# A hymba encoder block on one core: the negated row maxima added to the last three score pairs of a unit by accumulating DMAs, and the loads of q, K and V issued on the sync queue

## The chip, the cores and the metric

The kernel runs on one core of one Trainium2 chip. The metric is the device time of one execution in microseconds (us). The kernel before the change was run three times: the median is 2271.43 us, the lowest 2271.02 and the highest 2275.55. One further execution was profiled.

## The reference, cut to what matters

The program is one encoder layer for 2048 tokens and 16 meta tokens with a model width of 1024, all in float32. A projection of the normalised input gives queries (4 heads of 128), keys and values (2 heads of 128 each) and the input of a Fourier branch. The change lies in the attention of two query heads over one key and value head:

```python
def attend(qb):
    s = jnp.einsum('bkgqd,bksd->bkgqs', qb, kt).astype(jnp.float32) * scale
    p = jax.nn.softmax(s, axis=-1).astype(vt.dtype)
    return jnp.einsum('bkgqs,bksd->bkgqd', p, vt)
```

After that come the normalised outputs of attention and Fourier branch, an output projection added to the input, and a feed-forward part of width 4096.

## The kernel before, in words

A tile framework writes one queue of instructions for each engine: it takes the operations of the Python program, plans them by costs of its own, and so decides the order in which each engine runs them. On the chip each engine works through its queue strictly in that order and waits at an instruction until its operands are there. A change in one place can therefore move instructions on all engines.

Matrix products are mostly done three times over (helper `mm3`, lines 77 to 82): each operand is split into a high and a low part, and three products are added in one PSUM bank.

Attention runs beside the Fourier branch first (names `pa`, `py`, its last `py` at 497 us of the profiled span), then beside the output projection of the Fourier half (`pof`, 507 to 777 us), then beside that of the attention half (`poa`, 784 to 1019 us). It consists of 16 units; a unit is 256 queries of two heads, 512 columns, against all 2064 keys. The keys come in 16 tiles of 128 and one last tile of meta tokens.

- `scores(u, i)` makes one score tile on TensorE (PE) with three products, and ScalarE (ACT) copies it out of PSUM (line 780). Only two PSUM banks serve these tiles (`bufs=2`), so the third product from here waits for the copy of the first. Two tiles stand side by side in one pair `S` of 128x1024 in SBUF; a unit has eight pairs, 0 to 7. A running maximum `M` is kept on VectorE (DVE) at line 786.
- `stats(u)` turns the maxima of a unit into `mb`, the maximum of each of the 512 columns on all 128 partitions (line 811, a copy from PSUM on ACT).
- `softmax(u, i)` goes over the pairs: DVE subtracts `mb` from the pair (line 840), ACT takes the exponential (line 841), DVE adds the pair into `acc` (lines 845 and 847), and PE multiplies it by the values (line 849, name `o`, four matmuls a pair). These products of a unit stand in the order of the pairs.
- The scores run 20 tiles ahead of the softmax (`LEADT = 3` beyond one unit), so that `mb` of a unit is there about when the softmax of the unit before it ends.

The operands come from DRAM: `load_q` (line 738), `load_k` (704) and `load_v` (710 and 713), all issued by GpSimd (POOL). POOL also computes reciprocal square roots (line 192, names `rs_f`, `rs_m`, `rs_a`) and small additions (line 954). All other transfers of these stages are issued by the sync engine (SP): the tables of the Fourier branch (line 539, name `traw`), inputs, weights, and stores.

Of the kernel before, what the change touches and what calls it, by code (L numbers as in the profile page):

```python
# [13 lines left out]
AF = mybir.ActivationFunctionType  # L14
ALU = mybir.AluOpType
# [4 lines left out]
P = 128  # L20
# [11 lines left out]
NT = SEQ // P  # L32
# [3 lines left out]
MR = 96  # L36
# [13 lines left out]
P_BUFS = 5  # L50
S_BUFS = 11
A_BUFS = 5
ORDER = "1265734"
ISQ = 1.0 / math.sqrt(HD)


def f32v(ap):
    return ap.bitcast(F32)
# [26 lines left out]
def ins_of(x):  # L85
    return getattr(x, "ins", x)


def bc(ap, shape):
    return ap.broadcast_to(shape)  # L90
# [45 lines left out]
def encoder_block(ctx: ExitStack, tc: tile.TileContext, x, meta, w_in, w_f,  # L136
                  w_out, w_up, w_down, g_fin, g_cols, g_rows, c_id, c_rope, c_dft, c_even, c_odd, c_rem, out):
    nc = tc.nc
# [56 lines left out]
    q_d = [dram.tile([P, 2, NQ, 256], F32, name=f"q_d{b}") for b in range(8)]  # L195
    k_d = dram.tile([P, NKV, 2, SEQ + MR], F32, name="k_d")
    v_n = dram.tile([P, NKV, NT, P], F32, name="v_n")
    v_m = dram.tile([MR, NKV, P], F32, name="v_m")
    h_d = [dram.tile([P, D], F32, name=f"h_d{t}") for t in range(NT)]
    m_d = [dram.tile([P, KT, 512], F32, name=f"m_d{b}") for b in range(4)]  # L200
    f_d = {n: dram.tile([P, 2, 4, 512], F32, name=f"f_d{n}") for n in ORDER}

# [491 lines left out]
    def misc(name, shape=(P, 512)):  # L694
        return app.tile(list(shape), F32, name=name, tag="misc")


    KC = 4 * P
    KCP = 640

    def load_k(u, g, c):
        n = KC + (MR if c == 3 else 0)
        kt = ap.tile([P, 2, KCP if c == 3 else KC], R32, name=f"kt_{u}_{c}", tag=f"KT{c // 3}", bufs=1 if c == 3 else 3)
        nc.gpsimd.dma_start(kt[:, :, :n], k_d[:, g, :, c * KC:c * KC + n])
        return kt

    def load_v(u, g, c):
        if c == 4:
            vt = ap.tile([P, P], R32, name=f"vm_{u}", tag="VM", bufs=1)
            nc.gpsimd.dma_start(vt[:MR], v_m[:, g])  # L710
        else:
            vt = ap.tile([P, 4, P], F32, name=f"vn_{u}_{c}", tag="VT", bufs=4)
            nc.gpsimd.dma_start(vt, v_n[:, g, 4 * c:4 * c + 4])
        return vt

    o_d = [dram.tile([P, 2, NQ, 512], F32, name=f"o_d{b}") for b in range(4)]
# [12 lines left out]
    def attention():  # L729
# [5 lines left out]
        def load_q(u):  # L735
            b, g = units[u]
            q = ap.tile([P, 2, 2, 256], R32, name=f"q_{u}", tag="q", bufs=2)
            nc.gpsimd.dma_start(q, q_d[b][:, :, 2 * g:2 * g + 2])
            return q.rearrange("p l h n -> p l (h n)")

        def start(u, q=None):
            q = load_q(u) if q is None else q
            state[u] = dict(q=(q[:, 0], q[:, 1]), S=[], k=KV["k", u])
# [3 lines left out]
        def loads(kind, u, c):  # L747

            if u and units[u][1] == units[u - 1][1]:
                KV[kind, u] = KV[kind, u - 1]  # L750
            else:
                KV.setdefault((kind, u), []).append((load_v if kind == "v" else load_k)(u, units[u][1], c))
# [37 lines left out]
        def over_keys(x, name, op):  # L790

            ps = misc("pm_" + name, (P, 4, P))
            for a in range(4):
                nc.tensor.transpose(ps[:, a], x[:, a * P:(a + 1) * P], ident)
            r = ap2.tile([P, 4], F32, name="mx_" + name, tag="mx", bufs=2)
            nc.vector.tensor_reduce(r, ps, axis=AX.X, op=op)
            return r

        def rows_to_cols(vec, name):

            ps = misc("pd_" + name, (P, 4, P))
            for a in range(4):
                nc.tensor.transpose(ps[:, a], bc(vec[:, a:a + 1], [P, P]), ident)
            return ps.rearrange("p a e -> p (a e)")

        def stats(u):
            s = state[u]
            r = over_keys(s["M"], f"m{u}", ALU.max)
            yield
            mb = s["mb"] = ap2.tile([P, 512], F32, name=f"mb_{u}", tag="mb", bufs=2)  # L810
            nc.scalar.copy(mb, rows_to_cols(r, f"m{u}"))  # L811

        def softmax(u, i):

            s = state[u]
            nm = f"{u}_{i}"
            vt = KV["v", u]
            if i == NT:
                S = s["S"][-1][:MR]
                nc.vector.tensor_tensor(S, S, s["mb"][:MR], op=ALU.subtract)  # L820
                nc.scalar.activation(S, S, AF.Exp, scale=ISQ)
                hi = ap2.tile([P, 512], R32, name="ph_" + nm, tag="ph", bufs=1)
                acc = s["acc"]
                nc.scalar.copy(hi[:MR], S)
                nc.vector.tensor_tensor(hi[32:64], S[32:64], f32v(hi[32:64]), op=ALU.subtract)
                sm = s["sum"] = ap2.tile([P, 512], F32, name=f"sum_{u}", tag="pl", bufs=1)
                nc.vector.tensor_tensor(sm, acc[:, 0], acc[:, 1], op=ALU.add)
                nc.vector.tensor_tensor(sm[:META], sm[:META], S[:META], op=ALU.add)
                nc.tensor.matmul(s["O"], vt[4][:MR], hi[:MR], start=False, stop=True)
                return  # L830
            j = i // 2
            S = s["S"][j]
            if i == 0:
                s["acc"] = ap2.tile([P, 2, 512], F32, name=f"acc_{u}", tag="acc", bufs=1)
                s["O"] = app.tile([P, 512], F32, name=f"o_{u}", tag="O")
            acc = s["acc"]
            p = S
            if i % 2 == 0:
                mb = s["mb"].rearrange("p (o n) -> p o n", o=1).broadcast_to([P, 2, 512])
                nc.vector.tensor_tensor(S, S, mb, op=ALU.subtract)  # L840
                nc.scalar.activation(p, S, AF.Exp, scale=ISQ)  # L841
                return
            v = vt[j // 2]
            if j == 1:
                nc.vector.tensor_tensor(acc, s["S"][0], p, op=ALU.add)
            elif j > 0:
                nc.vector.tensor_tensor(acc, acc, p, op=ALU.add)
            for e in range(2):
                nc.tensor.matmul(s["O"], v[:, 2 * j % 4 + e], p[:, e], start=i + e == 1, stop=False)  # L849

        def finish(u):
# [25 lines left out]
            else:  # L877
                for h in range(2):
                    nc.vector.tensor_tensor(sqs[b], sqs[b], O[:, h * 256:(h + 1) * 256], op=ALU.add)

        q0 = load_q(0)
        for c in range(4):
            loads("k", 0, c)
# [7 lines left out]
        def more(upto):  # L891
            while ahead[0] < min(upto, total):
                w, i = divmod(ahead[0], K)
                if i == K // 2 and w < len(units) - 1:
                    start(w + 1)
                scores(w, i)
                loads_next("k", w, i)
                ahead[0] += 1
                if i == NT:
                    later.append(stats(w))  # L900
# [6 lines left out]
        for n in range(total):  # L907
            u, i = divmod(n, K)
            for g in list(later):
                if next(g, "end") == "end":  # L910
                    later.remove(g)
            softmax(u, i)
            loads_next("v", u, i)
            if i == NT:
                later.append(finish(u))
                next(later[-1])
            more(n + 1 + K + LEADT)
            yield
# [102 lines left out]
    def a_tile(name, dt=F32):  # L1021
        return mp.tile([P, 512], dt, name=name, tag="a", bufs=A_BUFS)

# [182 lines left out]
    def up_pass(p, sp, pc, UW, ready, first, hs, beside):  # L1206
# [8 lines left out]
        for g in range(8):  # L1215
            X, Y, p1, u2, p5, C = ({} for _ in range(6))

            def keep(name, q, t):
                nc.sync.dma_start(s_d[g // 2][:, ORDER.index(name), 2 * (g % 2) + q], t)

            for name in ORDER:
                hi, lo = ready.pop(0)
# [81 lines left out]
    def down_pass(p, sp, FIRST, hs):  # L1304
# [36 lines left out]
        def down_operands():  # L1341

            for g in range(4):
                raw, S, loads = {}, {}, []

                def stationary(name):
                    S[name] = []
                    for h in range(2):
                        r = dn.tile([P, 2, 512], F32, name=f"a{name}_{p}_{g}_{h}", tag="ar", bufs=a_bufs)
                        eng = nc.sync if g else nc.gpsimd  # L1350
                        loads[:] = [ins_of(eng.dma_start(r, s_d[g][:, ORDER.index(name), 2 * h:2 * h + 2]))]
                        S[name].append(r)
# [119 lines left out]
        for g in range(4):  # L1472
            X, Y = {}, {}
            last = g == 3
            for name in ORDER:
                (a0, b0), (a1, b1) = (lambda f: ((f[0], f[1]), (f[2], f[3])))(ready.pop(0))
# [255 lines left out]
```

## Time and profile before

| | before |
|---|---|
| median of 3 runs | 2271.43 us |
| the profiled execution's own time | 2272.19 us |
| its span, first to last instruction | 2270.4 us |
| PE busy | 2240.4 us |
| DVE busy | 1693.0 us |
| ACT busy | 1177.8 us |
| POOL busy | 248.0 us |
| clock granted to TensorE | 0.997 |

A time in the profile is counted from the first instruction of the span. "x" is how many instructions a group holds. In a group of instructions the mean length of one is given in ns, then the idle time of the engine ahead of them and what ended it. A matmul's row is longer than the time that it takes from the next one, since matmuls overlap: rows of 390 ns start 227 ns after each other. Rows with an engine's name and a q (SPq, POOLq) belong to that engine's queue, where transfers are issued.

### The profile page before, as it was taken

The numbers are of one execution on the slowest core, as the hardware profiler recorded it, in microseconds if no ns is written. First come the engines' busy times: TensorE is split into PE (matmuls) and PEld (weight loads), VectorE is DVE, ScalarE is ACT, GpSimd is POOL, SyncE is SP. The second block draws the span as 40 slices with busy tenths as digits, with TensorE's granted clock in tenths as the row PEclk, the third lists the DMA queues.
The fourth block names the chain that finished last, engine by engine and source line by source line (L and its number), as shares of the span: only waits on it lengthen the run. The fifth ranks groups of instructions, "written<-read, shape, count | busy, mean of one in ns | idle before, by whom it ended". The sixth has DMA issues, their size and how long they took to land.

```text
span 2270.4 us, 28121 instructions
## 1 busy us (share of the span) xinstructions
PE 2240.4 (99%) x10238; PEld 1774.5 (78%) x10238; DVE 1693.0 (75%) x2250; ACT 1177.8 (52%) x1997; POOL 248.0 (11%) x285
## 2 busy tenths in 40 slices
PE   9999999999999999999999999999999999999998
PEld 7888987766667666677888878888878888788887
DVE  6334589999999888888676669679655656696795
ACT  6443366665555566668555644334445555443343
POOL 2212120003223122010000020000200000200000
PEclk9999999999999999999999999999999999999999
DMA  5332252133343524367777575444674444864442
GB/s 203 89 107 77 78 157 81 51 94 113 101 155 116 192 90 136 126 254 243 254 233 237 201 275 192 158 133 149 227 311 166 156 151 155 306 201 157 128 138 84
DMA packets 191786, 367.40 MB, mean 162 GB/s; under 512 B 15760, under 2 KB 74768, under 8 KB 189984
## 3 DMA queue, kind: packets, MB, share of 16 engines
q1 hardware_dynamic: 171040, 310.08, 40.4%
q0 software_dynamic: 20464, 55.27, 7.7%
q8 instruction: 80, 1.31, 0.2%
q14 instruction: 58, 0.48, 0.1%
q10 hardware_dynamic: 144, 0.26, 0.0%
HBM read 236.28 MB, written 129.27 MB: 161 GB/s over the span
## 4 chain that ended last, share of the span: by engine, by line
PE 88%; DVE 7%; ACT 2%; issue 2%; POOL 1%; DMA 1%; POOLq 0%; DVEq 0%; ACTq 0%; SPq 0%
PE o L849 7%; PE ux L82 5%; PE ux L80 5%; PE ux L81 5%; PE dx L80 5%; PE dx L81 5%; PE dx L82 5%; PE uy L82 4%; PE uy L81 4%; PE uy L80 4%; PE dy L82 4%; PE dy L80 4%; PE dy L81 4%; PE s L80 2%; PE s L82 2%; PE s L81 2%
## 5 line engine op out<-in xcount | busy, mean ns | idle before, releaser
L849 PE MATMUL o<-S,vn 128*128 128x512 f32 x512 | 243.6, 596 | 4.2 <-ACT S L841 3.5
L70 ACT CAST ah<-a 128x1024 fp32r<-128x1024 f32 x108 | 112.9, 1050 | 259.8 <-PE dx L81 105.3
L80 PE MATMUL dx<-bh,ah 128*128 128x512 f32 x496 | 192.6, 388 | 1.3 <-DVE hs L1493 1.3
L780 ACT COPY S<-s 128x512 f32<-128x512 f32 x256 | 145.0, 584 | 91.9 <-PE s L82 72.5
L82 PE MATMUL dx<-bh,al 128*128 128x512 f32 x496 | 192.5, 388 | 0.0
L81 PE MATMUL dx<-bl,ah 128*128 128x512 f32 x496 | 192.5, 388 | 0.0
L80 PE MATMUL ux<-bf,wuh 128*128 128x512 f32 x448 | 176.0, 393 | 3.2 <-ACT wuh L70 3.1
L82 PE MATMUL ux<-bf,wul 128*128 128x512 f32 x448 | 175.4, 392 | 0.7 <-DVE wul L71 0.7
L81 PE MATMUL ux<-bf,wuh 128*128 128x512 f32 x448 | 175.4, 391 | 0.0
L840 DVE TENSOR_TENSOR S<-S,mb 128x1024 f32<-128x1024 f32 x128 | 155.2, 1227 | 11.8 <-ACT mb L811 11.7
L841 ACT ACTIVATE S<-S 128x1024 f32<-128x1024 f32 x128 | 135.1, 1063 | 43.3 <-DVE S L840 42.2
L80 PE MATMUL dy<-bh,ah 128*128 128x512 f32 (+1 forms) x388 | 151.5, 390 | 3.5 <-ACT ah L70 3.5
L82 PE MATMUL dy<-bh,al 128*128 128x512 f32 (+1 forms) x388 | 151.3, 390 | 1.6 <-DVE al L71 1.6
L71 DVE TENSOR_TENSOR al<-a,ah 128x1024 fp32r<-128x1024 f32 x108 | 131.1, 1220 | 27.2 <-ACT ah L70 26.9
L81 PE MATMUL dy<-bl,ah 128*128 128x512 f32 (+1 forms) x388 | 151.2, 390 | 0.0
L849 PEld LDWEIGHTS o<-S,vn 128*128 128x128 f32 x512 | 92.2, 189 | 75.1 <-issue 59.0
L80 PE MATMUL s<-q,kt 128*128 128x512 f32 (+1 forms) x272 | 145.1, 534 | 2.8 <-ACT S L780 2.4
L71 DVE TENSOR_TENSOR bl<-d,bh 128x1024 fp32r<-128x1024 f32 x92 | 112.1, 1219 | 21.5 <-ACT bh L70 21.5
L80 PE MATMUL uy<-bf,wuh 128*128 128x512 f32 x320 | 125.0, 391 | 0.3 <-ACT wuh L70 0.3
L82 PE MATMUL uy<-bf,wul 128*128 128x512 f32 x320 | 124.6, 390 | 0.7 <-DVE wul L71 0.7
L786 DVE TENSOR_TENSOR M<-M,S 128x1024 f32<-128x1024 f32 x96 | 117.6, 1225 | 9.9 <-ACT S L780 9.0
L81 PE MATMUL uy<-bf,wuh 128*128 128x512 f32 x320 | 124.8, 390 | 0.0
(323 smaller groups left out, 5663.2 us busy)
## 6 DMA issues: line engine op xcount, KB each, us to landing
a<-s_d SPq DMA_DIRECT2D x84, 512.0 KB, 3.7
R<-in_w_up_dram SPq DMA_DIRECT2D x32, 1024.0 KB, 5.5
s_d<-s SPq DMA_DIRECT2D x128, 256.0 KB, 2.1
s_d<-c SPq DMA_DIRECT2D x96, 256.0 KB, 2.8
d<-in_w_down_dram SPq DMA_DIRECT2D x48, 512.0 KB, 5.1
f_d<-lf SPq DMA_DIRECT2D x56, 256.0 KB, 2.8
bf<-f_d SPq DMA_DIRECT2D x7, 2048.0 KB, 13.5
a<-s_d POOLq DMA_DIRECT2D x24, 512.0 KB, 5.3
```

What stands on the lines that cost most here:

```text
L70: self.high = nc.scalar.copy(hi, src)
L71: self.low = nc.vector.tensor_tensor(lo, src, f32v(hi), op=ALU.subtract)
L80: nc.tensor.matmul(out, a[0], b[0], start=first, stop=False, skip_group_check=chain)
L81: nc.tensor.matmul(out, a[0], b[1], start=False, stop=False, skip_group_check=chain)
L82: nc.tensor.matmul(out, a[1], b[0], start=False, stop=last, skip_group_check=chain)
L780: nc.scalar.copy(S[:, i % 2], ps)
L786: nc.vector.tensor_tensor(M, M, S, op=ALU.max)
L840: nc.vector.tensor_tensor(S, S, mb, op=ALU.subtract)
L841: nc.scalar.activation(p, S, AF.Exp, scale=ISQ)
L849: nc.tensor.matmul(s["O"], v[:, 2 * j % 4 + e], p[:, e], start=i + e == 1, stop=False)
```

## The change

A constant `FAR = 5` is added. `mb` is now made with its sign turned, and added where it was subtracted. For the pairs 0 to 4 and for the last tile DVE does that as before. For the pairs 5, 6 and 7 DVE does nothing any more: `stats` issues three DMAs on POOL's queue that add `mb` into these pairs in SBUF, 512 KB of destination each, as soon as `mb` is there. The exponential of these pairs waits for its DMA. The loads of q, K and V go from POOL's queue to SP's.

```diff
+FAR = 5
 ...
-        nc.gpsimd.dma_start(kt[:, :, :n], k_d[:, g, :, c * KC:c * KC + n])
+        nc.sync.dma_start(f32v(kt[:, :, :n]), k_d[:, g, :, c * KC:c * KC + n])
 ...
-            nc.gpsimd.dma_start(vt[:MR], v_m[:, g])
+            nc.sync.dma_start(f32v(vt[:MR]), v_m[:, g])
 ...
-            nc.gpsimd.dma_start(vt, v_n[:, g, 4 * c:4 * c + 4])
+            nc.sync.dma_start(vt, v_n[:, g, 4 * c:4 * c + 4])
 ...
-            nc.gpsimd.dma_start(q, q_d[b][:, :, 2 * g:2 * g + 2])
+            nc.sync.dma_start(f32v(q), q_d[b][:, :, 2 * g:2 * g + 2])
 ...
-            nc.scalar.copy(mb, rows_to_cols(r, f"m{u}"))
+            nc.scalar.activation(mb, rows_to_cols(r, f"m{u}"), AF.Copy, scale=-1.0)
+            for S in s["S"][FAR:NT // 2]:
+                nc.gpsimd.dma_start(S, bc(mb.rearrange("p (o n) -> p o n", o=1), [P, 2, 512]), accum_op=ALU.add)
 ...
-                nc.vector.tensor_tensor(S, S, s["mb"][:MR], op=ALU.subtract)
+                nc.vector.tensor_tensor(S, S, s["mb"][:MR], op=ALU.add)
 ...
-                mb = s["mb"].rearrange("p (o n) -> p o n", o=1).broadcast_to([P, 2, 512])
-                nc.vector.tensor_tensor(S, S, mb, op=ALU.subtract)
+                if j < FAR:
+                    mb = bc(s["mb"].rearrange("p (o n) -> p o n", o=1), [P, 2, 512])
+                    nc.vector.tensor_tensor(S, S, mb, op=ALU.add)
                 nc.scalar.activation(p, S, AF.Exp, scale=ISQ)
```

With the change the planner also writes other orders. Two places matter below. A name such as `S_10_6424` is a pair by its first key tile (`S_10` is pair 5, `S_12` pair 6, `S_14` pair 7) with a serial number that only tells instances apart; in `s_4` the number is the key tile. The lines in the changed kernel are one to four higher: 780 is 781 there, 811 is 812, 841 is 845.

On ACT, from `mb` of unit 9 on (at 702.90 us in the profile of before), the kernel before has:

```order
L811 COPY mb_6565<-pd_m_6566 128x512
L780 COPY S_0_6541<-s_1_6575 128x512
L855 COPY O_6589<-o_6286 128x512
L780 COPY S_2_6595<-s_2_6591 128x512
L841 ACTIVATE S_0_6216<-S_0_6216 128x1024
L780 COPY S_2_6595<-s_3_6610 128x512
L841 ACTIVATE S_2_6248<-S_2_6248 128x1024
L841 ACTIVATE S_4_6318<-S_4_6318 128x1024
L70 CAST ohl_6649<-O_6589 128x512
L780 COPY S_4_6663<-s_4_6659 128x512
L780 COPY S_4_6663<-s_5_6667 128x512
```

And the changed kernel at the same place on ACT:

```order
L812 ACTIVATE mb_6565<-pd_m_6566 128x512
L781 COPY S_0_6541<-s_1_6578 128x512
L859 COPY O_6592<-o_6289 128x512
L781 COPY S_2_6598<-s_2_6594 128x512
L845 ACTIVATE S_0_6216<-S_0_6216 128x1024
L781 COPY S_2_6598<-s_3_6613 128x512
L845 ACTIVATE S_2_6251<-S_2_6251 128x1024
L845 ACTIVATE S_10_6424<-S_10_6424 128x1024
L845 ACTIVATE S_4_6321<-S_4_6321 128x1024
L845 ACTIVATE S_12_6465<-S_12_6465 128x1024
L71 CAST ohl_6652<-O_6592 128x512
L845 ACTIVATE S_14_6481<-S_14_6481 128x1024
```

The exponentials of the pairs 5, 6 and 7 have moved ahead of those of the pairs 2 to 4 and ahead of the copies of the next unit's score tiles 4 and 5, which follow in the next rows. In the kernel before, exponentials stand in the order of the pairs, and eleven copies of score tiles stand between `mb` and that of pair 7 in this unit; now there are three. The other units have moved in the same way: by the order, 9 to 19 such copies stood there in the units 0 to 14, now 3 to 5 and in unit 13 seven. The last unit has no copies behind it in either kernel.

On SP, before the first unit, the kernel before has stores and the tables of the Fourier branch:

```order
L454 DMA k_d<-kt_3398 512x1x96
L539 DMA traw_0_4049<-c_odd 128x516
L539 DMA traw_1_4055<-c_odd 128x516
L539 DMA traw_2_4061<-c_odd 128x516
L539 DMA traw_3_4067<-c_odd 128x516
```

And the changed kernel at the same place on SP:

```order
L455 DMA k_d<-kt_3398 512x1x96
L540 DMA traw_0_4052<-c_odd 128x516
L540 DMA traw_1_4058<-c_odd 128x516
L540 DMA traw_2_4064<-c_odd 128x516
L739 DMA q_3566<-q_d_102 128x2x512
L705 DMA kt_0_3568<-k_d 128x2x512
L705 DMA kt_1_3570<-k_d 128x2x512
```

The first loads of q and K, which stood at the head of POOL's queue, now stand behind three table loads on SP.

## The prediction

> **What bounds the kernel now.** I read the page first: busy times, the chain that ended last, the costliest groups.
>
> ```profile
> span 2270.4 us, 28121 instructions
> ...
> PE 2240.4 (99%) x10238; PEld 1774.5 (78%) x10238; DVE 1693.0 (75%) x2250; ACT 1177.8 (52%) x1997; POOL 248.0 (11%) x285
> ...
> PE 88%; DVE 7%; ACT 2%; issue 2%; POOL 1%; DMA 1%; POOLq 0%; DVEq 0%; ACTq 0%; SPq 0%
> ...
> L780 ACT COPY S<-s 128x512 f32<-128x512 f32 x256 | 145.0, 584 | 91.9 <-PE s L82 72.5
> ...
> L840 DVE TENSOR_TENSOR S<-S,mb 128x1024 f32<-128x1024 f32 x128 | 155.2, 1227 | 11.8 <-ACT mb L811 11.7
> L841 ACT ACTIVATE S<-S 128x1024 f32<-128x1024 f32 x128 | 135.1, 1063 | 43.3 <-DVE S L840 42.2
> ```
>
> TensorE is the bound: busy for 99% of the span and 88% of the chain. The share of DVE says nothing about single stages, so next I asked for the stretches of the span in which attention runs, and for the heavy stretch in which it starts.
>
> ```profile
> core 0: us, PE busy (x) PEld busy (x) DVE busy (x) ACT busy (x) POOL busy (x), PEclk, DMA share, GB/s
> 340.00:640.00 300.00, 295.21 (x1283) 202.96 (x1282) 293.29 (x364) 186.40 (x312) 56.37 (x54) 1.00 0.30 92
> 640.00:1000.00 360.00, 356.13 (x1429) 244.48 (x1428) 313.57 (x395) 217.82 (x357) 70.96 (x61) 1.00 0.41 137
> 320.00:340.00 20.00, 19.96 (x123) 17.48 (x122) 16.16 (x29) 15.47 (x30) 4.23 (x8) 1.00 0.98 293
> ```
>
> Between 340 and 640 us DVE is nearly as full as PE (293.3 against 295.2 of 300 us). The change takes load from it there. But PE is idle for only 4.8 us in the first stretch (300 - 295.21) and 3.9 us in the second (360 - 356.13): 8.7 us is about all that a lighter DVE can give.
>
> **The change part by part.** *DVE.* Three pairs in 16 units, 48 subtractions of 1.227 us, are 58.9 us of DVE work that goes. DVE is on the chain for 7%, but PE cannot get back more than its 8.7 us of gaps, and a part of these ends with POOL or with transfers. I take 5 us off, with 0 and 8.7 as bounds. The turned sign and additions in place of subtractions cost nothing: as many instructions of the same size.
>
> *The wait on ACT.* ACT works in order, and its order has changed: in unit 9 the exponentials of the pairs 5, 6 and 7 now stand right behind that of pair 1, each waiting for its DMA. So what counts is not when these pairs are needed, but what stands behind the waiting exponential: the copies of the next unit's scores. I work unit 9 out from its rows on ACT and PE.
>
> ```profile
> 702.90 0.59 ACT L811 COPY mb<-pd_m 128x512 f32<-128x512 f32 x1 [1.22 <-PE pd_m L803]
> ...
> 706.45 2.25 ACT L841 ACTIVATE S<-S 128x1024 f32<-128x1024 f32 x2
> 710.10 0.62 ACT L70 CAST ohl<-O 128x512 fp32r<-128x512 f32 x1 [1.39 <-DVE O L861]
> 711.26 1.27 ACT L780 COPY S<-s 128x512 f32<-128x512 f32 x2 [0.55 <-PE s L82]
> 709.97 0.79 PE L80 MATMUL s<-q,kt 128*128 128x512 f32 x1
> ...
> 711.06 0.40 PE L80 MATMUL s<-q,kt 128*128 128x512 f32 x1
> ...
> 711.75 1.88 PE L849 MATMUL o<-S,vn 128*128 128x512 f32 x4
> 713.07 0.79 PE L80 MATMUL s<-q,kt 128*128 128x512 f32 x1
> ```
>
> `mb` is ready at 703.5 and the exponential of pair 1 ends at 707.5 (706.45 + 1.06). The scores at 709.97, 711.06 and 713.07 are tiles 4, 5 and 6; tile 6 needs the bank of tile 4, copied at 711.26 to 711.85. When does an accumulating DMA land? No row of before has one. The nearest are plain transfers of the same 512 KB, with the us from issue to landing at the end:
>
> ```profile
> h_d<-xo SPq DMA_DIRECT2D x16, 512.0 KB, 2.7
> ...
> a<-s_d POOLq DMA_DIRECT2D x24, 512.0 KB, 5.3
> q<-q_d POOLq DMA_DIRECT2D x16, 512.0 KB, 4.6
> ...
> kt<-k_d POOLq DMA_DIRECT2D x15, 512.0 KB, 4.3
> ```
>
> POOL's plain loads take 4.3 to 5.3 us. A full stretch moved 293 GB/s, so 524,288 bytes take 1.8 us, and that is the distance of plain transfers in a row. An addition has to read the old values too: up to 1.8 us more for each. As an estimate I take 6.0 us from `mb` to the landing of pair 5 (between 4.3 and 5.3 + 1.8), and 2.7 us from one pair to the next (between 1.8 and 3.6).
>
> Then pair 5 lands at 709.5 and its exponential ends at 710.6, that of pair 2 at 711.6, just in time for the `o` at 711.75. Pair 6 lands at 712.2 (end 713.3), `ohl` ends at 713.9, pair 7 lands at 714.9 (end 716.0), and only then tile 4 is copied, until 716.5. Tile 6 starts at 716.5, not 713.07: PE stands still for 3.4 us in this unit. In unit 13 the exponential of pair 5 stands behind `ohl`, and those of the pairs 6 and 7 behind the copies of tile 7:
>
> ```profile
> 873.50 0.59 ACT L811 COPY mb<-pd_m 128x512 f32<-128x512 f32 x1 [0.33 <-PE pd_m L803]
> ...
> 883.47 0.64 ACT L70 CAST ohl<-O 128x512 fp32r<-128x512 f32 x1
> ...
> 887.34 1.28 ACT L780 COPY S<-s 128x512 f32<-128x512 f32 x2 [0.35 <-PE s L82]
> ```
>
> That is 10.0 and 14.5 us after `mb` (874.1), later than 6.0, 8.7 and 11.4, so nothing waits. By the order, units 4, 5, 9 and 11 are like unit 9 (three copies ahead of pair 7), ten units have four or five copies and I give them half, 1.7 us, and the last unit 2 us: 4 x 3.4 + 10 x 1.7 + 0 + 2 = 32.6, say 32 us.
>
> The Trainium skill, "Collectives: The Full Stack", section "The bandwidth ceiling: the fold count and why AG ≠ RS ≠ AR", says that an addition in a transfer reads two sources through one ring and comes out half as fast (62.28 against 32.35 GB/s there). By that rule the distance is the upper bound of 3.6 us, the pairs land at 6.0, 9.6 and 13.2, unit 9 loses 5.2 us (its copy would end at 718.3), and the sum would be about 17 us longer; no trace here shows an addition yet.
>
> *The start.* First q and K:
>
> ```profile
> 321.83 8.60 SPq L539 DMA_DIRECT2D traw<-c_odd  x4
> 314.06 0.92 POOL L738 DMA_DIRECT2D q<-q_d  x1
> 314.98 2.17 POOL L704 DMA_DIRECT2D kt<-k_d  x3
> 327.26 0.48 PE L80 MATMUL s<-q,kt 128*128 128x512 f32 x1
> ```
>
> They were issued at 314.06 on POOL; now three of the four table loads that begin at 321.83 go first on SP, the third about 325. Issued then, with 4.6 us to land, q comes no sooner than about 329.8, in a stretch whose engines were 98% busy. The first score stood at 327.26 and everything on PE comes after it: 2.5 us at least, twice that with the other traffic; I take 4. From unit 1 on SP is also passed by loads that wait for PE, with stores, tables and `h` queued behind them. I put this at 0: a chunk of K is asked for as soon as its slot is free, some 13 tiles ahead, and 272 tiles in the 660 us from 340 to 1000 make 2.4 us a tile, 31 us. Without that cover each late load costs PE its lateness.
>
> *POOL and the transfers.* 61 load issues go (20 of K, 25 of V, 16 of q), 48 come. What waits behind them on POOL is `rs_f`, `rs_m` and `rs_a`, for three issues of about 0.72 us (2.17 / 3 above): put at 0, bound 2.2 us a unit. 48 x 0.52 MB are 25 MB over 660 us, some 40 to 80 GB/s beside 92 and 137, at shares of 0.30 and 0.41: room enough.
>
> The sum goes against the profiled execution, 2272.19 us (1.8 more than its span): 2272.2 + 32 + 4 - 5 = 2303.2. The median lies 0.8 lower: **2302 us**, 1.3% slower.
>
> **The rivals.** *The additions land fast and DVE's relief is all there is.* If they land as fast as the store `h_d<-xo`, 2.7 us, with 0.72 us between them, at 706.2, 706.9 and 707.6, they are there when ACT comes by at 707.5; five instructions later tile 4 is copied until 713.0, and tile 6 starts at 713.07 as before. With all gaps closed and 2 us at the start: 2271.4 - 8.7 + 2 = 2265 us. For it speaks that the source lies in SBUF as that store's does; against it, that POOL's own transfers took 4.3 us or more. The Trainium skill, "DMA: Bandwidth & Descriptors", section "Anatomy of one DMA — SWDGE (gpsimd) path", fits 2.0 us plus bytes / 436e3 for DMAs issued by GpSimd; its estimate for 512 KB is 3.2 us, which would bring this rival's time. The rows above disagree with it by 1.1 to 2.1 us, and the measurement decides. It turns into a loss when pair 7 lands later than about 8 us after `mb`.
>
> *They land like plain loads* (4.6, 6.4, 8.2 us): tile 4 is then copied until 713.6 in unit 9, a stall of 0.5 us, about 5 us in all: 2271.4 + 5 + 4 - 5 = 2275 us, within 0.2% of no change.
>
> *They are slow*, 9.0 us with 4.5 between: pair 7 lands at 721.5, tile 6 starts at 723.2, 10.1 us late; with 4 x 10.1 + 10 x 7 + 6 = 116 us it is 2386 us.
>
> **How the numbers follow.** Forecast 0.56 (its own range 2285 to 2335, by landings of 5.3 to 7.1 us), fast 0.14, like plain loads 0.20, slow 0.10. A measurement can tell 0.2% (4.5 us) from no change. Faster: the fast rival, 0.14. Within: 0.12 of the plain one. Slower: 0.56 + 0.08 + 0.10 = 0.74. The range of 8 in 10 leaves out the slow rival's and half of the fast one's chance: 2264 to 2345 us.
>
> **What would show it.** Right: in the waits of the profile after, the exponential at line 845 waits for a DMA, some 2 to 4 us in most units and hardly in unit 13, copies of `s` wait behind it and PE's idle time between 340 and 1000 us grows from 8.7 to some 35 us. The issue rows give the landing: 6 to 11 us for the three. The first score starts near 331. Wrong: ACT hardly waits (landing under 5 us), or PE's idle time lies behind SP's loads instead.

## The result, and the profile after

| | before | after |
|---|---|---|
| median | 2271.69 us (4 runs, 2271.02 to 2275.55) | 2322.2 us (4 runs, 2320.11 to 2326.18) |
| span of the profiled execution | 2270.4 us | 2318.3 us |
| TensorE busy / idle in that span | 2240.4 / 30.0 us | 2250.8 / 67.5 us |
| clock granted to TensorE | 0.997 | 0.991 |

The changed kernel is slower by 2.2%: the ratio of the times is 1.0219, with a 95% interval of 1.0204 to 1.0235. The forecast was 2302 us with a range of 2264 to 2345 us. The sign, the place and the range held; the size was 20 us short. The span grew by 47.9 us, of which 37.5 us are idle time of TensorE and 10.4 us are time in which it was busy longer with the same 10238 matmuls.

From the page of the kernel after: the span, the busy times, and two groups of instructions that answer to groups of before.

```profile
span 2318.3 us, 28140 instructions
...
PE 2250.8 (97%) x10238; PEld 1781.4 (77%) x10238; DVE 1643.8 (71%) x2202; ACT 1178.1 (51%) x1997; POOL 242.0 (10%) x272
...
L81 PE MATMUL s<-q,kt 128*128 128x512 f32 (+1 forms) x272 | 150.0, 552 | 24.2 <-ACT S L781 20.5
...
L845 ACT ACTIVATE S<-S 128x1024 f32<-128x1024 f32 x128 | 133.4, 1065 | 76.9 <-DMA S<-mb 57.3
```

The scores of before, on its page:

```profile
L80 PE MATMUL s<-q,kt 128*128 128x512 f32 (+1 forms) x272 | 145.1, 534 | 2.8 <-ACT S L780 2.4
```

Read from the bottom up: the exponential (line 845) now has 76.9 us of idle time on ACT ahead of it, and 57.3 us of that end with a DMA that wrote `mb` into `S`. Before, it was 43.3 us, nearly all ended by DVE. One step on, the scores (line 81) have 24.2 us of idle time on TensorE ahead of them where they had 2.8, and 20.5 of it is ended by ACT's copy at line 781. DVE's busy time has fallen by 49 us (1693.0 to 1643.8), and TensorE waits more all the same.

The same two stretches as in the prediction, here 708 us together instead of 660, since nearly the whole loss falls into them, and the start of attention ahead of them:

```profile
core 0: us, PE busy (x) PEld busy (x) DVE busy (x) ACT busy (x) POOL busy (x), PEclk, DMA share, GB/s
320.00:340.00 20.00, 16.50 (x100) 14.63 (x99) 12.12 (x25) 11.84 (x23) 0.00 (x0) 0.91 1.02 327
340.00:660.00 320.00, 299.56 (x1300) 207.71 (x1299) 274.40 (x343) 192.21 (x319) 56.95 (x49) 0.99 0.50 126
660.00:1048.00 388.00, 366.60 (x1434) 250.26 (x1433) 287.59 (x372) 216.15 (x357) 71.92 (x63) 0.97 0.57 160
```

TensorE stands idle for 20.4 us in the second row (320 - 299.56) and 21.4 us in the third, 41.8 us where it was 8.7. The column after the engines is the clock: it was 1.00 in all three stretches of before and is 0.91, 0.99 and 0.97 now. The share of the transfer engines has gone from 0.30 and 0.41 to 0.50 and 0.57. (A packet counts whole in the stretch in which it begins, so a share can come out a little above 1.)

The place of the wait is the one that the prediction worked out, unit 9. Its rows on ACT from `mb` on, and then POOL's issue and TensorE's next score tile:

```profile
728.71 0.60 ACT L812 ACTIVATE mb<-pd_m 128x512 f32<-128x512 f32 x1 [1.23 <-PE pd_m L804]
...
736.27 2.01 ACT L845 ACTIVATE S<-S 128x1024 f32<-128x1024 f32 x2 [2.91 <-DMA S<-mb]
738.80 1.06 ACT L845 ACTIVATE S<-S 128x1024 f32<-128x1024 f32 x1 [0.52 <-DMA S<-mb]
...
741.34 1.06 ACT L845 ACTIVATE S<-S 128x1024 f32<-128x1024 f32 x1 [0.98 <-DMA S<-mb]
742.30 0.57 ACT L781 COPY S<-s 128x512 f32<-128x512 f32 x1
...
729.72 3.71 POOL L814 DMA_DIRECT2D S<-mb  x3 [0.59 <-ACT mb L812]
...
742.92 0.50 PE L81 MATMUL s<-q,kt 128*128 128x512 f32 x1 [3.48 <-ACT S L781]
...
744.49 0.63 PE L83 MATMUL pof<-wfh,yl 128*128 128x512 f32 x1
744.92 0.63 PE L81 MATMUL pof<-wfh,yh 128*128 128x512 f32 x1
```

`mb` ends at 729.3. The three additions have landed 7.0, 9.5 and 12.0 us later (736.27, 738.80 and 741.34 are the starts of the waiting exponentials); assumed were 6.0, 8.7 and 11.4. The copy of the next score tile at 742.30 stands behind the last, and TensorE stands still for 3.48 us; worked out were 3.4. That the two are so near is in part luck: the last landing was 0.6 us later than assumed, and TensorE too came to the tile some 0.6 us later, 10.1 us after `mb` (742.92 - 3.48 - 729.3) where it was 9.6 in before. The last two rows show what was not worked out: matmuls that started 0.23 us after each other start 0.43 us after each other once TensorE has stood still.

The clock record of the trace gives five stretches between 320 and 1048 us in which half the clock was granted, each a multiple of 3.41 us long; before had none there. TensorE in exactly these stretches:

```profile
330.80:334.20 3.40, 3.08 (x7) 2.48 (x8) 0.59 (x1) 0.73 (x2) 0.00 (x0) 0.50 1.05 405
518.60:525.40 6.80, 4.85 (x9) 3.16 (x10) 5.36 (x6) 6.67 (x15) 1.65 (x2) 0.50 0.59 189
743.80:747.20 3.40, 3.40 (x10) 2.61 (x9) 3.35 (x4) 1.56 (x3) 0.00 (x0) 0.51 0.11 27
795.00:798.40 3.40, 3.40 (x9) 2.61 (x8) 3.40 (x5) 1.27 (x3) 0.00 (x0) 0.51 0.96 259
839.40:853.10 13.70, 9.77 (x18) 5.91 (x19) 8.51 (x11) 10.74 (x15) 1.46 (x1) 0.50 0.60 147
sum 30.70, PE 24.50 PEld 16.77 DVE 21.20 ACT 20.97 POOL 3.11; mean PE 4.90 PEld 3.35 DVE 4.24 ACT 4.19 POOL 0.62
```

24.5 us of busy time at half the clock are 12.2 us lost. Behind attention, before the last microseconds, before has 10.2 us at half clock and after 6.8 us, which gives 1.7 us back: 10.5 us, and TensorE's busy time grew by 10.4.

### The profile page after: what moved, and what is told of

Read it like the earlier page. It is cut to its first block, busy times and chain, and to the rows that moved or that the text cites. A ratio compares the mean times of both kernels' runs of the same rounds, so it can differ in the third digit from the quotient of the medians.

```text
span 2318.3 us, 28140 instructions
## 1 busy us (share of the span) xinstructions
PE 2250.8 (97%) x10238; PEld 1781.4 (77%) x10238; DVE 1643.8 (71%) x2202; ACT 1178.1 (51%) x1997; POOL 242.0 (10%) x272
## 4 chain that ended last, share of the span: by engine, by line
PE 67%; issue 5%; DMA 5%; DVE 4%; ACT 2%; POOL 1%; POOLq 0%; ACTq 0%; DVEq 0%
PE ux L83 5%; PE ux L81 5%; PE ux L82 5%; PE dx L81 5%; PE dx L82 5%; PE dx L83 5%; PE o L853 5%; DMA S<-mb 4%; PE uy L83 4%; PE uy L81 4%; PE uy L82 4%; PE dy L83 4%; PE dy L81 4%; PE dy L82 4%; PE s L81 1%
## 5 line engine op out<-in xcount | busy, mean ns | idle before, releaser
L71 ACT CAST ah<-a 128x1024 fp32r<-128x1024 f32 x108 | 112.9, 1050 | 259.0 <-PE dx L82 94.5
L81 PE MATMUL s<-q,kt 128*128 128x512 f32 (+1 forms) x272 | 150.0, 552 | 24.2 <-ACT S L781 20.5
L845 ACT ACTIVATE S<-S 128x1024 f32<-128x1024 f32 x128 | 133.4, 1065 | 76.9 <-DMA S<-mb 57.3
L1216 ACT ACTIVATE c<-c 128x512 f32<-128x512 f32 x96 | 60.5, 632 | 122.5 <-DVE c L1263 119.6
```

Source lines behind the costliest of these rows:

```text
L71: self.high = nc.scalar.copy(hi, src)
L81: nc.tensor.matmul(out, a[0], b[0], start=first, stop=False, skip_group_check=chain)
L1216: nc.scalar.activation(dst, src, AF.Relu)
```

## The experiments

The theory (A) is: ACT works in order, waits at exponentials that stand early in its queue for additions that land late, the copies of the next scores stand behind, TensorE stands idle and is then given half the clock for some microseconds. The rivals: the loads on the sync queue are late (B), POOL's queue holds something up (C), or the additions cost by the transfers and the SBUF that they share (D). Medians are of runs beside runs of the kernel before on the same chip; the ratio is that to the kernel before.

| run | median us | ratio | 95% interval |
|---|---|---|---|
| after | 2322.2 | 1.0219 | 1.0204 to 1.0235 |
| loads only | 2273.07 | 0.9999 | 0.9989 to 1.0008 |
| additions only | 2317.85 | 1.0190 | 1.0174 to 1.0205 |
| pair order | 2271.93 | 0.9994 | 0.9984 to 1.0004 |
| relief only | 2268.88 | 0.9978 | 0.9968 to 0.9988 |
| plain copies | 2280.97 | 1.0044 | 1.0030 to 1.0057 |
| one pair | 2285.11 | 1.0057 | 1.0043 to 1.0071 |
| busy start | 2271.43 | 0.9998 | 0.9989 to 1.0007 |
| pair order, first loads on POOL | 2266.08 | 0.9978 | 0.9969 to 0.9987 |
| pair order, all loads on POOL | 2269.75 | 0.9988 | 0.9979 to 0.9997 |
| pair order, first loads on POOL, two pairs | 2265.06 | 0.9960 | 0.9948 to 0.9973 |

**The loads alone.** The changed kernel with

```diff
-FAR = 5
+FAR = 8
```

> The loads of q, K and V on the sync queue as in the changed kernel, no addition by DMA (FAR = 8): DVE adds the negated maxima to all pairs, and the orders of ACT and DVE are those of the kernel before but for the first unit. Theory A (ACT waits at the early exponentials for late additions, TensorE stands still behind it and is then given half the clock for some us; the loads cost only the start): 3.5 us of idle time ahead of the first score, one stretch of 3.4 us at half clock behind it (1.7 us lost), nothing later, so about 2276 us (2274 to 2279). Rival B (the loads on the sync queue come late behind stores, tables and loads that wait, in all units): over 2290 us, with TensorE waiting for kt, q or vn at several places between 340 and 1000 us.

The first two rows are from TensorE's timeline at the start, the others from the stretches.

```profile
331.68 0.77 PE L81 MATMUL s<-q,kt 128*128 128x512 f32 x1 [4.13 <-DMA kt<-k_d]
332.24 0.63 PE L82 MATMUL s<-q,kt 128*128 128x512 f32 x1
```

```profile
320.00:340.00 20.00, 15.87 (x91) 13.97 (x91) 10.42 (x24) 10.21 (x20) 0.00 (x0) 0.83 0.99 317
340.00:640.00 300.00, 297.31 (x1297) 205.37 (x1296) 293.73 (x362) 189.04 (x315) 34.93 (x25) 1.00 0.28 93
640.00:1000.00 360.00, 358.24 (x1435) 245.55 (x1434) 314.88 (x399) 219.32 (x361) 53.68 (x38) 1.00 0.39 135
```

The wait for `kt` and the half clock are there (4.1 us idle, the clock at 0.83 in that stretch), yet the time is that of before. Much of what was lost comes back: TensorE's idle time between 340 and 1000 us is 2.7 + 1.8 = 4.5 us where before had 8.7. The likely reason is that DVE is nearly as full as TensorE there (293.73 against 297.31 us in the first stretch), so that a TensorE that starts later waits less for what DVE feeds; no run shows this by itself. B falls: TensorE waits for no load in any later unit.

**The additions alone.** The loads of q, K and V go back to POOL's queue.

```diff
-            nc.sync.dma_start(vt, v_n[:, g, 4 * c:4 * c + 4])
+            nc.gpsimd.dma_start(vt, v_n[:, g, 4 * c:4 * c + 4])
```

(and the same at the other three loads)

> The additions by DMA as in the changed kernel, the loads of q, K and V back on POOL's queue; the orders of PE, DVE and ACT are nearly those of the changed kernel. Theory A: the start is that of the kernel before, and the waits at the early exponentials stay: about 2317 us (2308 to 2326), 30 us or more of idle TensorE between 340 and 1048 us, several stretches of it at half clock. Rival B (the loads on the sync queue are the larger part): under 2295 us. Rival C (what costs is that the loads now stand behind or ahead of the additions on POOL's queue): over 2330 us here, with waits for kt or vn.

```profile
L81 PE MATMUL s<-q,kt 128*128 128x512 f32 (+1 forms) x272 | 149.3, 549 | 22.0 <-ACT S L781 22.0
...
L845 ACT ACTIVATE S<-S 128x1024 f32<-128x1024 f32 x128 | 133.6, 1065 | 67.5 <-DMA S<-mb 52.2 <-DVE S L844 15.1
```

Nearly the whole loss stays, with the same waits: 52.2 us of ACT's time end with the additions, 22.0 us of TensorE's with ACT's copies. C falls too. The rest to the changed kernel (1.0219 - 1.0190, 6.6 us, with intervals that overlap by a hair) is about what the start costs where it is not given back (4 to 6 us, further down). ACT's waits for the additions differ by 5 us as well (57.3 against 52.2), so that it is the start alone is not shown.

**The exponentials in the order of the pairs.** One edge more for the planner, additions and loads as in the changed kernel:

```diff
-                nc.scalar.activation(p, S, AF.Exp, scale=ISQ)
+                with tc.issue_after(s["exp"]) if j > 0 else nullcontext():
+                    s["exp"] = ins_of(nc.scalar.activation(p, S, AF.Exp, scale=ISQ))
```

> The changed kernel, with one edge more: the exponential of each pair may be placed only behind that of the pair before it. The additions by DMA and the loads stay. On ACT 5 to 14 copies of score tiles then stand between the maxima and the exponential of pair 5, where 2 to 5 stood, which is some 12 us or more. Theory A: the additions have landed when ACT comes by, its waits for them fall from 57 us to under 8 us, the stretches at half clock between 340 and 1048 us are gone, and the time is the start's 5 us above the kernel before, less up to 8.7 us of DVE relief: 2268 to 2280 us. Rival D (the additions cost by themselves, by the SBUF and the transfer engines that they share with the copies and loads): over 2300 us even in this order.

```profile
L81 PE MATMUL s<-q,kt 128*128 128x512 f32 (+1 forms) x272 | 151.4, 557 | 6.9 <-ACT S L781 3.4 <-DMA kt<-k_d 3.4
...
L846 ACT ACTIVATE S<-S 128x1024 f32<-128x1024 f32 x128 | 132.5, 1062 | 27.0 <-DVE S L844 26.2
```

No group of ACT's waits ends with an addition any more, and the whole loss of 50 us is gone, with the same 48 additions on the same queue, landing as late (a median of 8.3 us in both). That is the decisive run: A holds, and D falls as the main cause. One item of the expectation failed: a stretch at half clock is left near 514 us, behind this:

```profile
513.27 0.72 ACT L74 ACTIVATE wfh<-wfr,cols 128x512 fp32r<-128x512 f32 x1 [4.49 <-DMA wfr<-in_w_out_dram]
...
514.51 0.80 PE L81 MATMUL s<-q,kt 128*128 128x512 f32 x1 [3.40 <-ACT S L781]
```

A weight load (`wfr`) lands late in a stretch in which the transfer engines are full (a share of 1.08 between 500 and 515 us, where the run with the loads alone has 0.67). So a small part of D is real.

**DVE's relief alone.** No addition for the pairs 5 to 7, by anyone:

```diff
-                nc.gpsimd.dma_start(S, bc(mb.rearrange("p (o n) -> p o n", o=1), [P, 2, 512]), accum_op=ALU.add)
+                pass
 ...
-                nc.scalar.activation(p, S, AF.Exp, scale=ISQ)
+                nc.scalar.activation(p, S, AF.Exp, scale=ISQ if j < FAR else 0.01 * ISQ)
```

> The maxima of the pairs 5, 6 and 7 are added by nobody: neither by DVE nor by DMA. The exponential of these pairs takes a hundredth of the score, so that it stays finite; everything else is as in the changed kernel, the loads on the sync queue too. This gives the relief of DVE (48 operations of 1.2 us) without a wait. If TensorE's gaps were due to DVE, it gains up to 8.7 us over the run with the loads alone: about 2268 us. If the gaps end with POOL or transfers, nothing: about 2276 us, the same as the loads alone.

It is faster than the loads alone by 0.9999 - 0.9978, 4.8 us; the forecast took 5. The planner put the exponentials of these pairs earlier still here, ahead of `mb`, so early exponentials that wait for nothing show no cost.

**Plain copies instead of additions.**

```diff
-                nc.gpsimd.dma_start(S, bc(mb.rearrange("p (o n) -> p o n", o=1), [P, 2, 512]), accum_op=ALU.add)
+                nc.gpsimd.dma_start(S, bc(mb.rearrange("p (o n) -> p o n", o=1), [P, 2, 512]))
```

> The changed kernel with the three DMAs of a unit as plain copies of the negated maxima into the pairs 5, 6 and 7: the same bytes written, the same queue, the same order on every engine, but nothing is added, so the scores of these pairs are left out. Theory A with an addition that reads the old values too and so takes longer: the landing falls from 8.3 us to 4 to 6 us, ACT's wait for these DMAs from 57 us to under 30 us, and the time lies between 2280 and 2300 us. Rival: issue on POOL (1.7 us each) and the bytes written set the landing, not the addition: landing about 8 us and about 2318 us as in the changed kernel.

The issues on POOL (mean ns), and the landings: first the changed kernel's, then those of the plain copies.

```profile
L814 POOL DMA_DIRECT2D S<-mb x48 | 59.4, 1717 | 237.9 <-ACT mb L812 190.6 <-DVE tlo L549 31.8 <-DVE S L823 15.4
...
S<-mb POOLq DMA_DIRECT2D x48, 512.0 KB, 8.3
```

```profile
L814 POOL DMA_DIRECT2D S<-mb x48 | 35.0, 732 | 234.2 <-ACT mb L812 191.1 <-DVE tlo L549 30.4 <-DVE S L823 12.6
...
S<-mb POOLq DMA_DIRECT2D x48, 512.0 KB, 4.6
...
L845 ACT ACTIVATE S<-S 128x1024 f32<-128x1024 f32 x128 | 132.8, 1064 | 33.7 <-DMA S<-mb 16.9 <-DVE S L844 16.4
```

With the same order on every engine and the same bytes written, the record of an issue is 0.73 us long where that of an addition is 1.72 (the three of a unit overlap and keep POOL for 2.2 and 3.7 us), a plain copy lands in 4.6 us where an addition takes 8.3, and ACT waits 16.9 us for it instead of 57.3. The loss falls from 50 to 10 us (0.44%). So four fifths of the loss hang on what an addition takes more than a copy.

**One pair by DMA instead of three.**

```diff
-FAR = 5
+FAR = 7
```

> FAR = 7: only pair 7 gets its maxima by DMA, pairs 5 and 6 by DVE as before; the loads stay on the sync queue. Theory A: one landing a unit instead of three in a row, issued first and so about 7 us after the maxima; the exponential of pair 7 still comes early in ACT's order, but there is one wait where there were three. About a third of the loss: 2280 to 2292 us. If the first landing of a unit is what costs and the other two hide behind it: over 2300 us. If one early addition is hidden: about 2272 us.

```profile
L845 ACT ACTIVATE S<-S 128x1024 f32<-128x1024 f32 x128 | 133.8, 1063 | 52.7 <-DVE S L844 29.8 <-DMA S<-mb 22.2
```

A third of the additions, a quarter of the loss (0.57%), and 22.2 us of ACT's waits instead of 57.3: the cost goes about with the number. The landing was shorter than expected, 5.1 us at the median, with no other addition ahead.

**The clock.** The run with the loads alone, and in the gap at its start 30 transposes whose result is not used:

```diff
+        busy = misc("busy", (P, 4, P))
+        with tc.issue_after(KV["at"]):
+            for n in range(30):
+                nc.tensor.transpose(busy[:, n % 4], ident, ident)
```

(`KV["at"]` is the first load of q.)

> The run with the loads alone, and 30 transposes of the identity on TensorE between the last product of pa and the first score, where it stood idle for 4.1 us and was then given half the clock for 6.8 us; their result is not used. The transfers at that place stay as they are. Theory of the clock (it is halved where TensorE has stood idle for some 3 us): the first score waits as long as before, but no stretch at half clock follows between 320 and 345 us. Rival (the load of the transfers, at a share of 0.99, or the return of the wide matmuls halves it): a stretch of 3.4 to 6.8 us at half clock is there as before. The time of the whole, 2271 to 2274 us, can hardly tell them apart.

```profile
327.41 3.44 PE L892 MATMUL busy<-ident 128*128 128x128 f32 x30
331.21 0.47 PE L81 MATMUL s<-q,kt 128*128 128x512 f32 x1 [0.36 <-DMA kt<-k_d]
331.52 0.39 PE L82 MATMUL s<-q,kt 128*128 128x512 f32 x1
```

```profile
320.00:340.00 20.00, 19.64 (x136) 17.92 (x135) 13.30 (x26) 12.96 (x25) 0.00 (x0) 1.00 1.01 324
```

The first score waits for the same load and starts at 331.2, under transfers as full as before (a share of 1.01), and the clock stays at 1.00: the scores behind the first follow each other every 0.23 us instead of 0.43. It is the idle time that halves the clock. The time of the whole (2271.43 against 2273.07 us) can't tell the two apart, as expected. The Trainium skill, "TensorE: Matmul & The Clock Gate", section "What's actually happening", says that the array falls to half its clock after an idle window of about 3.4 us and comes back after a busy one, the windows running freely; the stretches of 3.41, 6.83 and 13.65 us here agree. How much idle time it takes, the traces tell (last section).

**Is there a version that beats both?** The pair order, with the first loads of q and K on POOL's queue:

```diff
-        nc.sync.dma_start(f32v(kt[:, :, :n]), k_d[:, g, :, c * KC:c * KC + n])
+        (nc.sync if u else nc.gpsimd).dma_start(f32v(kt[:, :, :n]), k_d[:, g, :, c * KC:c * KC + n])
 ...
-            nc.sync.dma_start(f32v(q), q_d[b][:, :, 2 * g:2 * g + 2])
+            (nc.sync if u else nc.gpsimd).dma_start(f32v(q), q_d[b][:, :, 2 * g:2 * g + 2])
```

> The exponentials in the order of the pairs as in the run of that name, and the first loads of q and K (unit 0) back on POOL's queue, all later ones on the sync queue. Theory A: no idle time and no half clock ahead of the first score, no waits for additions, DVE relieved by 59 us: 2265 to 2270 us, 0.1 to 0.3% faster than before. If the start is given back later anyway (the run with the loads alone was no slower than before): the same as in pair order, about 2272 us.

2266.08 us, as expected. That is 5.9 us less than the pair order by the medians and 3.6 us by the ratios (0.9994 - 0.9978), with intervals that overlap by a hair. The start, which cost nothing measurable with DVE full, costs some 4 to 6 us once DVE is relieved.

The pair order with all loads on POOL's queue (the edits of the additions alone and of the pair order together, so nothing of the load move):

> The additions by DMA with the exponentials in the order of the pairs, and all loads of q, K and V on POOL's queue as in the kernel before: the additions without any part of the load move. If the move of the later loads to the sync queue is worth nothing by itself: 2266 us, the same as with only unit 0 on POOL. If POOL's 1.7 us issues hold up loads of K or V, or these hold up the additions: TensorE waits for kt or vn, over 2272 us.

2269.75 us lies between the two expectations, and its interval overlaps with that of the run before it. No wait of TensorE for `kt` or `vn` shows; whether the later loads gain by the sync queue stays open.

And with only two pairs by DMA:

```diff
-FAR = 5
+FAR = 6
```

> The fastest version so far (pair order, first loads on POOL's queue) with FAR = 6: only the pairs 6 and 7 get their maxima by DMA. If the idle time of 3.3 us near 506 us and the half clock behind it come from the additions' share of the transfer engines (a load of wfr lands late there), fewer additions shorten it: 2262 to 2266 us. If DVE's relief is what gains, a third of it less: 2266 to 2269 us.

```profile
340.00:640.00 300.00, 297.48 (x1299) 205.86 (x1298) 281.27 (x354) 191.24 (x318) 55.63 (x44) 1.00 0.45 123
640.00:1000.00 360.00, 359.92 (x1460) 250.16 (x1460) 295.43 (x383) 218.62 (x362) 59.63 (x54) 1.00 0.55 169
...
504.82 0.72 ACT L74 ACTIVATE wfh<-wfr,cols 128x512 fp32r<-128x512 f32 x1 [1.72 <-DMA wfr<-in_w_out_dram]
```

The lowest time: 2265.06 us, 0.40% below before (0.27 to 0.52%); from the same version with three pairs (0.22%) the intervals don't quite separate it. ACT's wait for `wfr` is 1.72 us where it was 4.49 in the pair order, no stretch at half clock is left in attention, and TensorE's idle time between 340 and 1000 us is 2.5 + 0.1 = 2.6 us.

## Why the prediction was right, and where its sizes were off

**The wait on ACT (32 us): right in mechanism, near in size.** The gaps of over 0.8 us in TensorE's timeline after, added up by the unit in whose additions they lie, against the forecast:

| units | forecast | measured |
|---|---|---|
| 9 | 3.4 us | 3.5 us |
| 4, 5, 11 | 3.4 us each | 6.4, 4.7, 6.8 us |
| the ten at half (0 to 3, 6 to 8, 10, 12, 14) | 17 us | 17.1 us, from 0 to 4.4 us each |
| 13 | 0 | 0 |
| 15 | 2 us | 2.2 us |

In all 40.8 us where 32.6 stood. The ten units agree only as a sum: six of them lose 1.5 to 4.4 us and four nothing. Nearly the whole excess is in the units 4, 5 and 11. In 4 and 11 the additions met other transfers, and there the step that failed is "room enough". In unit 5 almost no other transfer ran between `mb` and the last landing, and the pairs landed 5.7, 9.6 and 12.1 us after `mb`; what was wrong is that its loss was taken over from unit 9. A copy of `O` stands between its waiting exponentials on ACT, and TensorE stood still for 1.6 us for that copy and for 3.1 us at the products `o`. Unit 11 shows the transfers: six loads of `h` go out on SP from 821 to 827 us, just ahead of `mb` (827.4), the last three of them here:

```profile
825.20 1.57 SPq L1042 DMA_DIRECT2D h<-h_d  x3
```

```profile
832.00:838.00 6.00, 4.50 (x19) 2.73 (x17) 2.34 (x3) 0.00 (x0) 0.00 (x0) 1.00 1.09 298
...
839.31 2.00 ACT L845 ACTIVATE S<-S 128x1024 f32<-128x1024 f32 x2 [7.57 <-DMA S<-mb]
```

The engines are full (1.09), the first addition is there 11.9 us after `mb` and not 6.0, and ACT waits 7.57 us at one instruction. The mean shares of the stretches, 0.30 and 0.41 before, said nothing about this moment. The distance from one landing to the next was short, too: 2.7 us were taken, 2.5 were measured in unit 9, but 3.0 at the median of all units and 5.4 at most.

**The clock: missing from the sum.** The prediction counted the microseconds in which TensorE stands still and not what follows them, 10.4 us of slower matmuls. This is the largest part of the 20 us that were short. It also flatters an estimate. The Trainium skill, "Collectives: The Full Stack", section "The bandwidth ceiling: the fold count and why AG ≠ RS ≠ AR", says that an addition in a transfer comes out half as fast as a copy. By that rule the prediction's sum would have been 17 us longer, which comes close to the measured time, but 10.4 us of the measured loss are the clock's. The rule's ratio agrees with the runs: at the median of all units the additions landed 3.0 us after each other and the plain copies 1.5, in unit 9 2.5 and 1.3. The 3.6 us do not, since they are twice 1.8 us, and 1.8 us, taken from the rate of a full stretch, was too long for a plain transfer here.

**The start (+4 us): right in place, its price depends on what else waits.** The first score stood at 331.12 (forecast: near 331), 3.5 us idle, and then half clock. Alone it costs nothing measurable, since much of it is given back between 340 and 1000 us; with DVE relieved it costs some 4 to 6 us.

**DVE (-5 us): right in size, alone.** 4.8 us where nothing else waits. The reason for taking only a part of the 8.7 us does not hold: by the waits of before, none of TensorE's gaps between 340 and 1000 us ends with POOL or with a transfer, 6.6 us end with ACT and 1.6 with DVE. In the changed kernel nothing of the gain shows, and the likely reason is that ACT's waits take the place of these gaps (36.7 of TensorE's 41.8 us end with an exponential or a copy of a score tile on ACT): the forecast subtracted it from waits that it could not shorten.

In sum: the idle time was to grow by 32 + 4 - 5 = 31 us and grew by 37.5, and the 10.4 us of the clock were not in it. Of the rivals, landing like plain loads came true where the DMAs were plain copies: 2280.97 us there, against 2275 worked out. The slow rival overstated the distance (4.5 us, measured 3.0 at the median). The bound of 2.2 us a unit for the issues on POOL was too low, since the three kept it for 3.7 us. That they hold up `rs_f`, `rs_m` and `rs_a` was not tried by itself; in pair order the same issues leave no loss.

## What to carry to other kernels

An operation that is moved from a busy engine to a DMA frees that engine, but its consumer now waits inside an in-order queue: look at what the planner put behind the consumer, not at when the result is needed. One ordering edge was worth the whole 50 us here, and turned the loss into a gain once the start was mended. Price a stall on TensorE at its length plus what the halved clock takes behind it, and price a transfer by the share of the transfer engines at its moment, not by the mean of the stage.

## What the runs showed of the hardware

- An accumulating DMA of 512 KB from SBUF to SBUF has an issue of 1.72 us on POOL and a plain copy of the same bytes one of 0.73 us; they landed after 8.3 and 4.6 us at the median, which holds waiting for each other and for other transfers. The first of a unit, with little beside it, took 5.2 and 3.2 us in nine of the sixteen units (3.2 is the estimate that the prediction set aside for the longer medians of loads). In the shares of the transfer engines, 24 additions between 340 and 640 us raise 0.28 (loads alone) to 0.53 (pair order), 0.25 x 300 / 24 = 3.1 us of all engines for each; plain copies raise it to 0.39, 1.4 us each.

```profile
340.00:640.00 300.00, 295.02 (x1293) 206.04 (x1292) 271.31 (x341) 189.46 (x315) 56.78 (x49) 0.99 0.53 134
```

```profile
340.00:640.00 300.00, 293.82 (x1288) 204.10 (x1287) 271.36 (x340) 189.84 (x314) 47.82 (x49) 1.00 0.39 134
```

  The column GB/s stands at 134 for both: a DMA that adds keeps the engines busy 2.2 times as long for the same bytes that it counts.
- Half the clock came behind idle times of TensorE that were shorter than the 3.41 us of its stretches, too, and not behind every longer one. Two scores of the run with the additions alone, each after an idle time, and the 3.4 us behind each:

```profile
684.78 0.74 PE L81 MATMUL s<-q,kt 128*128 128x512 f32 x1 [2.02 <-ACT S L781]
...
737.69 0.50 PE L81 MATMUL s<-q,kt 128*128 128x512 f32 x1 [3.53 <-ACT S L781]
```

```profile
684.90:688.30 3.40, 3.40 (x10) 2.75 (x11) 2.92 (x3) 2.59 (x4) 0.00 (x0) 0.50 1.01 216
737.70:741.10 3.40, 3.40 (x15) 2.81 (x16) 2.85 (x4) 1.56 (x4) 0.00 (x0) 1.00 0.23 81
```

  Behind 2.02 us of idle time the clock is 0.50 and 10 matmuls run; behind 3.53 us it is 1.00 and 15 run. A gap counts by where it falls: in each of the twelve traces all changes of the clock lie on one grid of 3.413 us. The windows of this grid that hold the two gaps:

```profile
681.46:684.87 3.41, 1.39 (x6) 0.66 (x4) 1.29 (x3) 2.61 (x4) 0.07 (x1) 1.00 1.10 187
732.66:736.07 3.41, 1.50 (x4) 0.38 (x2) 0.88 (x2) 1.90 (x3) 0.61 (x1) 1.00 0.98 184
736.07:739.49 3.42, 1.80 (x8) 1.49 (x9) 2.19 (x3) 3.13 (x5) 0.00 (x0) 1.00 0.68 213
```

  The gap of 2.02 us lies in one window, in which TensorE is busy for 1.39 of 3.41 us (41%); that of 3.53 us is cut by an edge of the grid and leaves 44% and 53%. Between 320 and 1050 us this divides all windows of the twelve traces without exception: each of the 22 windows at full clock with TensorE busy for 41% or less was followed by one at half clock, and none with 44% or more was. From half clock, windows with 74% or less were followed by another at half clock, those with 86% or more by one at full clock. Later in the kernels, with other matmuls, the two kinds of windows at full clock overlap between 43 and 53%. This was read off the finished traces; no run moved a gap across an edge of the grid to try it.
